# Embedding projection in plain fp32 between the out-projection's outputs, its operands split earlier, norm roots taken on token rows

## The chip, the cores and the metric

The kernel runs on one core of a Trainium2 chip. The metric is the device time of one execution, in microseconds (us). The engines are TensorE (PE; weight loads are listed apart as PEld), VectorE (DVE), ScalarE (ACT), GpSimd (POOL) and SyncE (SP), whose queue issues nearly all DMA transfers in program order.

## The reference

Two layers of a decoder trunk for 1024 prompt tokens and 8 x 4 sample tokens with the same weights, all in float32. Each layer, cut to what matters here:

```python
# layer 0: o = gated linear attention(rms_norm(x)); layer 1: o = dilated window attention
x = x + o @ w_o                                  # out-projection, 1024 x 1024
h = rms_norm(x, g_f)
x = x + (silu(h @ w_gate) * (h @ w_up)) @ w_fo   # SwiGLU, hidden width 22 x 128
h = rms_norm(x, g_e)
x = x + sigmoid(h @ w_eg) * (p[layer] @ w_ep)    # p: 256 numbers per token; w_ep: 256 x 1024
```

## The kernel before

All activations lie transposed: 8 k-tiles of 128 features (partitions) by T = 1056 tokens, so a tile is 128x1056 and a matmul takes one 128x128 weight tile and a third of the tokens, 352 columns. For accuracy each operand of the large products is split into a high and a low part in the format fp32r (`split`: ACT casts the high part, DVE subtracts for the low part), and a product takes three matmuls: high by high, high by low, low by high (`XH,whi`, `XL,whi`, `XH,wlo`). The few plain float32 matmuls (`ones` by `ssq`, transposes) take their operands unsplit.

`block` runs once per layer, in stages:

- The out-projection comes in two halves of four k-tiles each. The first half (`mix_out`, or the end of `mixer` in layer 1) runs while attention still finishes on other engines; its sums with the residual go to DRAM (`Xp`). For the second half the operands O4 to O7 are loaded (`ot`) and split, and the sums come back as `X[m]`. Eight outputs m, in the order 0, 4, 1, 5, 2, 6, 3, 7, take 36 matmuls each. `second` adds an output to X, stores it (`Xr`), squares it into `ssq` and scales it by the norm's weight.
- `gated` computes SwiGLU's hidden tiles by a seven-product scheme after Strassen: a 2x2 split of weights (`seven_weights`) and tokens (`seven_tokens`, after every output m > 3, for the pair k = m - 4 and m). Each of 22 hidden tiles takes 7 products (`al`, `be`, `ga`) of 24 matmuls of 264 columns. Before the first of them stands `norm_done`: the sum over features as a matmul of `ones` by `ssq`, then root and reciprocal on all 128 partitions.
- The down projection takes the hidden tiles back from DRAM (`Gd`, loaded into `gr`) in chunks of 4, 4, 4, 4, 3, 3. In the last chunk X is renormed on the way (`renorm`, `square_sum`).
- The gate stage: `w_eg` by X, eight outputs of 72 matmuls, times the embedding projection `embed(m)`: 18 matmuls from split `p` (pH, pL) and split `w_ep`. Three embeds stand in the last chunk (`EP_AT`), five in the gate stage.

Tiles come from rotating pools, and a scheduler orders the instructions of each engine ahead of time; each engine then runs its own list in order, and semaphores hold an instruction until its operands are there and its buffer is free.

Of the kernel before, what the change touches and what calls it, by code (L numbers as in the profile page):

```python
# [8 lines left out]
F32 = mybir.dt.float32  # L9
# [26 lines left out]
def yoco_step_kernel(  # L36
# [62 lines left out]
    rstd = const.tile([128, T], F32, name="rstd")  # L99

# [21 lines left out]
    Xp = [dr.tile([128, T], F32, name=f"Xp{k}") for k in range(KT)]  # L122
# [21 lines left out]
    def seven_weights(pool, src1, src2):  # L144
# [15 lines left out]
        nc.vector.tensor_tensor(s2, s1, a11, op=ALU.subtract)  # L160
        out[6] = parts(6, s2)
        nc.vector.tensor_tensor(s3, a11, a21, op=ALU.subtract)
        out[7] = parts(7, s3)
        out[5] = parts(5, s1)
        out[4] = parts(4, a22)
        nc.vector.tensor_tensor(s4, a12, s2, op=ALU.subtract)
        out[3] = parts(3, s4)
        return out


    def seven_tokens(x1, x2, tiles, temp):
        a, b = slice(0, HT), slice(HT, T)
        t12, t34 = temp("t12"), temp("t34")
        nc.vector.tensor_tensor(t12[:, a], x1[:, b], x1[:, a], op=ALU.subtract)
        nc.vector.tensor_tensor(t12[:, b], x2[:, b], t12[:, a], op=ALU.subtract)
        bo = tiles("B1")
        split(bo[:, a], bo[:, b], x1[:, a])
        out = {1: (bo[:, a], bo[:, b])}
        nc.vector.tensor_tensor(t34[:, a], x2[:, b], x1[:, b], op=ALU.subtract)
        nc.vector.tensor_tensor(t34[:, b], x2[:, a], t12[:, b], op=ALU.subtract)  # L180
        for x, n1, n2 in ((t12, 5, 6), (x2, 2, 3), (t34, 7, 4)):
            hi, lo = tiles("Bh"), tiles("Bl")
            split(hi, lo, x)
            out[n1], out[n2] = (hi[:, a], lo[:, a]), (hi[:, b], lo[:, b])
        return out
# [354 lines left out]
    def mix_out(half, src, w_o, hl, get, evac, other=None):  # L540
        H_, L_ = hl
        for k in range(4):
            t = get("ot")
            nc.sync.dma_start(t, src[4 * half + k])
# [7 lines left out]
    def gated(i, pool, X7, temp):  # L552

        with ExitStack() as st:
# [9 lines left out]
            for j in range(NH):  # L564
                w = seven_weights(pool, w_fi[i, j], w_fi[i, NH + j])
# [22 lines left out]
    def block(i, sx, src, w_o, gla_scope=None):  # L588
        def first(m, s, ps):
            x = et("xf")  # L590
            nc.sync.dma_start(x, x_t[m])
            nc.vector.tensor_tensor(v3(x), ps, v3(x), op=ALU.add)
            nc.sync.dma_start(Xp[m], x)

        if gla_scope is not None:
            st, et, rest = gla_scope
            mix_out(0, src, w_o, (XH, XL), et, first, (AFTER, rest))
            st.close()
        xp = sx.enter_context(tc.tile_pool(name="xp", bufs=8, side="right"))
        sb, sw = ExitStack(), ExitStack()  # L600
        bg = sb.enter_context(tc.tile_pool(name="bg", bufs=12, side="right"))
        w7 = sw.enter_context(tc.tile_pool(name="w7", bufs=1))
# [4 lines left out]
        def bt(name, dtype=F32):  # L607
            return bg.tile([128, T], dtype, tag="b", name=name)

        X = {}  # L610
        ssq, X7 = bt("ssq"), {}

        def second(m, s, p):
# [4 lines left out]
            if m == 0:  # L618
                nc.scalar.activation(ssq, X[m], AF.Square)
            else:  # L620
                t = bt("sq")
                nc.scalar.activation(t, X[m], AF.Square)
                nc.vector.tensor_tensor(ssq, ssq, t, op=ALU.add)
            nc.scalar.activation(X[m], X[m], AF.Copy, scale=gcol(G_F[i] + m))
            if m > 3:
                k = m - 4
                if k == 3:
                    norm_done(ssq)
                left = [7, 0, 7, 2][k]

                def tile_(name):
                    nonlocal left
                    left -= 1
                    return xtile(name) if left >= 0 else bt(name, F32R)

                X7[k] = seven_tokens(X[k], X[m], tile_, xt if k else bt)

        H_, L_ = ([xtile(f"O{a}{k}") for k in range(4)] for a in "HL")
        for k in range(4):
            t = xtile("ot", F32)  # L640
            nc.sync.dma_start(t, src[4 + k])
            split(H_[k], L_[k], t)
        for m in range(KT):
            X[m] = xt(f"X{m}")
            nc.sync.dma_start(X[m], Xp[m])
        for m in (0, 4, 1, 5, 2, 6, 3, 7):
            for s, p in pieces(wtile(w_o[m][:, 512:], 4), H_, L_, m == 7):
                second(m, s, p)
# [3 lines left out]
        gated(i, w7, [X7[k] for k in range(4)], xt)  # L652
# [8 lines left out]
        X = [xt(f"X{m}") for m in range(KT)]  # L661
        pe = {}

        def embed(m):
            ps = proj(wtile(w_ep[i, m], 2), pH, pL)
            pe[m] = tmp("pe")
            nc.scalar.copy(v3(pe[m]), ps)

        m0 = 0
        for n in FCH:  # L670
            last = m0 + n == NH
            GH, GL = [], []
            for a in range(n):
                t = tmp("gr")
                nc.sync.dma_start(t, Gd[m0 + a])
                GH.append(bt("GH", F32R) if last else xtile("GH"))
                GL.append(bt("GL", F32R) if last else xtile("GL"))
                split(GH[a], GL[a], t)
            if m0 == 0:
                for m in range(KT):  # L680
                    nc.sync.dma_start(X[m], Xr[m])
            if last:
                new_x()
                pH, pL = ([bt(a, F32R) for _ in range(2)] for a in ("pH", "pL"))
                for k in range(2):
                    t = tmp("pt")
                    nc.sync.dma_start(t, p_t[i, k])
                    split(pH[k], pL[k], t)
            for m in range(KT):
# [7 lines left out]
                if last and m in EP_AT:  # L697
                    embed(EP_AT.index(m))
# [4 lines left out]
        for m in range(KT):  # L703
            if m not in pe:
                embed(m)
# [11 lines left out]
        sb.close()  # L717
# [356 lines left out]
    def mixer(mq):  # L1074

        with ExitStack() as st:
# [13 lines left out]
            hp = st.enter_context(tc.tile_pool(name="hp", bufs=1, side="right"))  # L1090
            H_ = [hp.tile([128, T], F32R, name=f"OH{k}") for k in range(4)]
            L_ = [hp.tile([128, T], F32R, name=f"OL{k}") for k in range(4)]
            for k in range(4):
                t = hp.tile([128, T], F32, tag="ot", name="ot", bufs=4)
                nc.sync.dma_start(t, Ad[k])
                split(H_[k], L_[k], t)
            for m in range(KT):
                x = hp.tile([128, T], F32, tag="xf", name="xf", bufs=4)
                nc.sync.dma_start(x, Xd[m])
                for c, ps in mx.proj(wtile(w_ob[m][:, :512], 4), H_, L_):  # L1100
                    s = slice(c * CW, (c + 1) * CW)
                    nc.vector.tensor_tensor(x[:, s], ps, x[:, s], op=ALU.add)
                nc.sync.dma_start(Xp[m], x)


    open_products()
    open_x()
    scope = gla(*load_x())
    sx = ExitStack()
    X, ssq, tp = block(0, sx, Od, w_oa, gla_scope=scope)  # L1110
# [3 lines left out]
    mixer(mq)  # L1114
    mq_stack.close()
    open_products()
    open_x()
    block(1, sx, Ad, w_ob)
    sx.close()
    xh_stack.close()  # L1120
# [116 lines left out]
```

## Time and profile before

| what | value |
|---|---|
| median of 3 runs | 3000.31 us (2995.72 to 3001.23) |
| the profiled execution | 3000.49 us |
| its span | 2998.7 us |
| PE busy | 2902.7 us, 97% |
| DVE busy | 1866.5 us, 62% |
| ACT busy | 1095.9 us, 37% |
| mean DMA rate | 97 GB/s |
| mean granted clock of TensorE | 0.988 |

The span runs from the first to the last instruction; the rest of the time lies around it. PE bounds the kernel as a whole, so what can be saved lies in its instructions and in the places where it waits. The granted clock is a share of 2.4 GHz: 0.50 is 1.2 GHz, the lower of TensorE's two levels.

### The profile page before, as it was taken

Reading aid. Unit: us, or ns where it says so; the run is one execution under the profiler, and the core shown is the slowest. Engines: PE = TensorE matmul, PEld = TensorE weight load, DVE = VectorE, ACT = ScalarE, POOL = GpSimd, SP = SyncE. Lnnn points to the kernel's source line nnn. Section 1 sums busy time; section 2 is a strip of 40 time slices with the busy share of each in tenths; the row PEclk is TensorE's granted clock in tenths of the full one; section 3 lists DMA queues with packets and bytes.
Section 4 is the critical chain, followed back from the end, with each engine's and each line's share of the span. In section 5 each row is a group of like instructions: output and inputs, shape, how many; then the busy total and the mean of one; then the engine's idle time right before and its main releaser. Section 6 shows DMA issues by size and latency. Waiting matters only on the chain.

```text
span 2998.7 us, 47341 instructions
## 1 busy us (share of the span) xinstructions
PE 2902.7 (97%) x19956; PEld 2770.8 (92%) x19956; DVE 1866.5 (62%) x2787; ACT 1095.9 (37%) x1777; POOL 20.3 (1%) x44
## 2 busy tenths in 40 slices
PE   8999998899999999999999999988899999999999
PEld 7889898899999999999988889887799999999999
DVE  6344455866666444557687778773876666545363
ACT  5333343422222221335455555552532222222142
POOL 0000000000000000000000000000000000000000
PEclk9999999999999999999999999999999999999999
DMA  3121245222222532122433141336222222343112
GB/s 128 58 73 50 73 140 208 93 79 86 72 79 82 188 113 64 54 77 90 132 95 107 54 121 43 114 109 236 100 79 79 86 72 79 128 153 104 45 61 77
DMA packets 133989, 291.08 MB, mean 97 GB/s; under 512 B 34160, under 2 KB 58736, under 8 KB 132752
## 3 DMA queue, kind: packets, MB, share of 16 engines
q1 hardware_dynamic: 133040, 287.72, 29.1%
q8 instruction: 157, 2.57, 0.4%
q14 instruction: 56, 0.46, 0.1%
q10 hardware_dynamic: 736, 0.33, 0.0%
HBM read 216.14 MB, written 71.86 MB: 96 GB/s over the span
## 4 chain that ended last, share of the span: by engine, by line
PE 85%; DVE 8%; DMA 3%; ACT 2%; issue 1%; SPq 0%; DVEq 0%; ACTq 0%
PE mm L239 39%; PE be L194 12%; PE ga L194 8%; PE al L194 8%; PE mm L869 6%; PE p_s L916 1%; PE mm L257 1%; PE p_o L984 1%; DVE q L741 1%; DVE hs L749 1%; DVE hs L750 1%; DVE q L751 1%; DVE Bl L134 1%; PE p_u L467 1%; PE p_us L485 1%
## 5 line engine op out<-in xcount | busy, mean ns | idle before, releaser
L133 ACT CAST whi<-raw 128x1024 fp32r<-128x1024 f32 (+3 forms) x260 | 203.9, 784 | 815.2 <-PE mm L239 580.7
L134 DVE TENSOR_TENSOR wlo<-raw,whi 128x1024 fp32r<-128x1024 f32 (+3 forms) x260 | 231.2, 890 | 75.4 <-ACT whi L133 75.2
L239 PE MATMUL mm<-XH,whi 128*128 128x352 f32 x1200 | 271.3, 331 | 0.4 <-ACT q_in L263 0.4
L239 PE MATMUL mm<-XL,whi 128*128 128x352 f32 x1200 | 265.4, 327 | 0.0
L239 PE MATMUL mm<-XH,wlo 128*128 128x352 f32 x1200 | 264.0, 326 | 0.0
L692 DVE TENSOR_TENSOR X<-mm,X 128x1056 f32<-128x1056 f32 (+1 forms) x100 | 121.1, 1212 | 218.4 <-PE mm L239 218.4
L239 PE MATMUL mm<-GH,whi 128*128 128x352 f32 x1038 | 225.3, 326 | 10.7 <-ACT GH L133 10.7
L133 ACT CAST hw<-S 128x512 fp32r<-128x512 f32 x176 | 109.3, 622 | 329.1 <-PE ga L194 181.0
L239 PE MATMUL mm<-GL,whi 128*128 128x352 f32 x1038 | 224.5, 325 | 0.0
L239 PE MATMUL mm<-GH,wlo 128*128 128x352 f32 x1038 | 224.1, 324 | 0.0
L194 PE MATMUL be<-Bh,lw 128*128 128x264 f32 x1056 | 216.2, 286 | 5.9 <-DVE lw L134 5.9
L194 PE MATMUL be<-Bh,hw 128*128 128x264 f32 x1056 | 216.4, 286 | 1.8 <-ACT hw L133 1.7
L194 PE MATMUL be<-Bl,hw 128*128 128x264 f32 x1056 | 216.7, 287 | 0.0
L239 PEld LDWEIGHTS mm<-XH,whi 128*128 128x128 f32 x1200 | 205.3, 189 | 9.1 <-issue 2.5
L239 PEld LDWEIGHTS mm<-XL,whi 128*128 128x128 f32 x1200 | 205.3, 189 | 3.2 <-issue 1.3
L239 PEld LDWEIGHTS mm<-XH,wlo 128*128 128x128 f32 x1200 | 204.1, 189 | 2.2 <-issue 1.6
L869 PE MATMUL mm<-XL,whi 128*128 128x352 f32 x576 | 193.6, 336 | 0.0
L869 PE MATMUL mm<-XH,whi 128*128 128x352 f32 x576 | 193.2, 335 | 0.0
L869 PE MATMUL mm<-XH,wlo 128*128 128x352 f32 x576 | 188.9, 328 | 0.0
L239 PEld LDWEIGHTS mm<-GH,whi 128*128 128x128 f32 x1038 | 177.8, 190 | 11.7 <-ACT GH L133 11.7
L239 PEld LDWEIGHTS mm<-GL,whi 128*128 128x128 f32 x1038 | 177.4, 189 | 0.5 <-DVE GL L134 0.4
L239 PEld LDWEIGHTS mm<-GH,wlo 128*128 128x128 f32 x1038 | 177.1, 189 | 0.0
(340 smaller groups left out, 6212.7 us busy)
## 6 DMA issues: line engine op xcount, KB each, us to landing
raw<-in_w_fi_dram SPq DMA_DIRECT2D x88, 512.0 KB, 3.5
Gd<-g SPq DMA_DIRECT2D x44, 528.0 KB, 2.7
gr<-Gd SPq DMA_DIRECT2D x44, 528.0 KB, 4.7
raw<-in_w_fo_dram SPq DMA_DIRECT2D x64, 256.0 KB, 2.7
raw<-in_w_a_dram SPq DMA_DIRECT2D x24, 512.0 KB, 3.5
raw<-in_w_q_dram SPq DMA_DIRECT2D x24, 512.0 KB, 3.8
kk<-in_ck_dram SPq DMA_DIRECT2D x40, 256.0 KB, 3.2
vv<-in_cv_dram SPq DMA_DIRECT2D x40, 256.0 KB, 3.0
```

The source lines that it names most:

```text
L133: nc.scalar.copy(hi, x)
L134: nc.vector.tensor_tensor(lo, x, hi.bitcast(F32), op=ALU.subtract)
L194: nc.tensor.matmul(ps[:, c, :HC], a[:, k, :], b[:, c * HC:(c + 1) * HC], start=(first and k == 0 and i == 0), stop=(k == len(xs) - 1 and i ...
L239: nc.tensor.matmul(ps[:, c, :CW], a[:, k, :], b[k][:, c * CW:(c + 1) * CW], start=(k == 0 and i == 0), stop=(k == n - 1 and i == 2),)
L257: nc.tensor.matmul(ps, a[:, k, :], b[k][:, s], start=(k == 0 and i == 0), stop=(k == n - 1 and i == 2))
L467: nc.tensor.matmul(p, kr[:, j], vt[:, j], start=True, stop=True)
L485: nc.tensor.matmul(p, kr[q, 8], vm[q], start=True, stop=True, tile_position=(16 * j, 0))
L692: nc.vector.tensor_tensor(like(X[m], s, p), p, like(X[m], s, p), op=ALU.add)
L741: nc.vector.scalar_tensor_tensor(dst[:, :NP].rearrange("p (r u) -> p u r", r=4)[:, u], q[:, :e].rearrange("p (u r) -> p u r", r=4), g, t[: ...
L749: nc.vector.stream_shuffle(t[32:64], dst[:32], [(a + 16) % 32 for a in range(32)])
L750: nc.vector.tensor_tensor(t[:32], t[32:64], tab[32:64], op=ALU.mult)
L869: nc.tensor.matmul(ps, a[:, k, :], b[k][:, s], start=(k == 0 and i == 0), stop=(k == n - 1 and i == 2))
```

## The change

- `embed(m)` takes the raw `w_ep` and the raw `p`, as six plain float32 matmuls of 352 columns, and stands behind the outputs of the out-projection's second half: two behind the first, one behind each of the next six, none behind the last. ACT copies it out, it goes to DRAM (`Pd`) and comes back in the gate stage (`load_pe`). The embeds in the last chunk and the gate stage go.
- The first half's sums stay in SBUF: `first_half` and `mixer` open X's pool themselves; `Xp` goes.
- O4, O5 and O6 are loaded and split at the end of the first half (`out_split`). O7 follows at the second half's beginning.
- `norm_spread` takes the place of `norm_done` ahead of SwiGLU: nine matmuls of `ssq` blocks by one column of ones give the sums with tokens on partitions (128x9, `p_c`); root and reciprocal run on that (`rcol`); nine matmuls of `ones` by diagonal matrices (`dg`) spread them over 128 partitions (`p_r`), and ACT copies them into `rstd`.
- `seven_weights` and `seven_tokens` become generators, so that the first hidden tile's operands are made in pieces: the token sums one output later than before (`later`), the weights around the last output and the norm.
- The first chunk's four G tiles are loaded into X's pool (`GS`) before the SwiGLU weights' pool is released. In the mixer the O tiles are staged in the queries' buffers (tag `q`).

```diff
+    def norm_spread(ssq, dg, n=D):
+        blocks = [(j, min(128, T - 128 * j)) for j in range(9)]
+        p = sm.tile([128, 9], F32, tag="sm", name="p_c")
+        for j, m in blocks:
+            nc.tensor.matmul(p[:m, j:j + 1], ssq[:, 128 * j:128 * j + m], ones[:, :1], start=True, stop=True)
+        for r, c in ((slice(0, 128), slice(0, 8)), (slice(0, 32), slice(8, 9))):
+            nc.scalar.activation(rcol[r, c], p[r, c], AF.Sqrt, scale=1.0 / n, bias=epsb[r])
+            nc.vector.reciprocal(rcol[r, c], rcol[r, c])
+        nc.vector.tensor_tensor(dg[:, :NP].rearrange("p (j n) -> p j n", j=8), ident[:, None, :].to_broadcast([128, 8, 128]),
+                                rcol[:, :8, None].to_broadcast([128, 8, 128]), op=ALU.mult)
+        nc.vector.tensor_tensor(dg[:32, NP:], ident[:32, :32], rcol[:32, 8:9].to_broadcast([32, 32]), op=ALU.mult)
+        for g in range(3):
+            s = slice(512 * g, min(T, 512 * g + 512))
+            q = sm.tile([128, 512], F32, tag="sm", name="p_r")[:, :s.stop - s.start]
+            for j, m in blocks[4 * g:4 * g + 4]:
+                nc.tensor.matmul(q[:, 128 * j - s.start:128 * j - s.start + m], ones[:m], dg[:m, 128 * j:128 * j + m], start=True, stop=True)
+            nc.scalar.copy(rstd[:, s], q)
...
+    def first_half(et, rest):
...
         for m in range(KT):
-            for s, p in pieces(wtile(w_o[m][:, half * 512:half * 512 + 512], 4), H_[:4], L_[:4], half == 1 and m == 7):
-                evac(m, s, p)
-            if other and m == other[0]:
-                other[1]()
+            nc.sync.dma_start(X[m], x_t[m])
+            for s, p in pieces(wtile(w_oa[m][:, :512], 4), H_, L_, False):
+                nc.vector.tensor_tensor(v3(X[m]), p, v3(X[m]), op=ALU.add)
+            if m == AFTER:
+                rest()
+        for k in range(3):
+            out_split(Od[4 + k], H2[k], L2[k], et)
+        return xp, X, H2, L2
...
+        L_ = L_ + [lt("OL7", F32R)]
+        out_split(src, H_[3], L_[3], lt)
+        ps_ = [lt(f"p{k}") for k in range(2)]
+        for k in range(2):
+            nc.sync.dma_start(ps_[k], p_t[i, k])
...
+        def embed(m):
+            raw = raws.tile([128, 1024], F32, tag="raw", name="raw")
+            nc.sync.dma_start(raw[:, :256], w_ep[i, m])
+            ps = mm.tile([128, 3, 512], F32, tag="mm", name="mm")
+            for k in range(2):
+                for c in range(3):
+                    nc.tensor.matmul(ps[:, c, :CW], raw[:, 128 * k:128 * k + 128], ps_[k][:, c * CW:(c + 1) * CW],
+                                     start=(k == 0), stop=(k == 1))
+            t = lt("pe")
+            nc.scalar.copy(v3(t), ps[:, :, :CW])
+            nc.sync.dma_start(Pd[8 * i + m], t)
...
+        for n, m in enumerate((0, 4, 1, 5, 2, 6, 3, 7)):
+            w = wtile(w_o[m][:, 512:], 4)
+            if n == 7:
+                weights = seven_weights(w0, w7, w_fi[i, 0], w_fi[i, NH])
+                next(weights)
+            for s, p in pieces(w, H_, L_, n == 7):
+                second(m, s, p)
+            if later is not None:
+                for _ in tokens(later):
+                    pass
+                later = None
             if m > 3:
...
+                later = m - 4
+            for e in ((0, 1), (2,), (3,), (4,), (5,), (6,), (7,), ())[n]:
+                embed(e)
+        last = tokens(3)
+        next(last)
+        next(last)
+        dg = xt("dg")
+        norm_spread(ssq, dg)
+        next(weights)
+        next(last)
+        next(weights)
...
+        GS = []
+        for a in range(FCH[0]):
+            t = xt("gr")
+            nc.sync.dma_start(t, Gd[a])
+            GS.append(t)
         sw.close()
...
             for k in range(4):
-                t = hp.tile([128, T], F32, tag="ot", name="ot", bufs=4)
-                nc.sync.dma_start(t, Ad[k])
-                split(H_[k], L_[k], t)
+                out_split(Ad[k], H_[k], L_[k], lambda name: mx.pool.tile([128, T], F32, tag="q", name=name, bufs=QB))
```

The order on PE in layer 0's second half. In the kernel before, one output ends and the next begins like this (OH_3720 to OH_3723 are O4 to O7, high parts; each row is three column pieces):

```order
L239 MATMUL mm<-OH_3722,wlo 128x352 x3
L239 MATMUL mm<-OH_3723,whi 128x352 x3
L239 MATMUL mm<-OL_3727,whi 128x352 x3
L239 MATMUL mm<-OH_3723,wlo 128x352 x3
L239 MATMUL mm<-OH_3720,whi 128x352 x3
L239 MATMUL mm<-OL_3724,whi 128x352 x3
```

In the changed kernel the same place reads as follows (OH_3321 to OH_3324 are O4 to O7; p_3752 and p_3753 are the two k-tiles of p):

```order
L271 MATMUL mm<-OL_3327,whi 128x352 x3
L271 MATMUL mm<-OH_3323,wlo 128x352 x3
L271 MATMUL mm<-OH_3324,whi 128x352 x3
L271 MATMUL mm<-OL_3747,whi 128x352 x3
L271 MATMUL mm<-OH_3324,wlo 128x352 x3
L671 MATMUL mm<-p_3752,raw 128x352 x3
L671 MATMUL mm<-p_3753,raw 128x352 x3
L271 MATMUL mm<-OH_3321,whi 128x352 x3
```

An embed of six plain matmuls has moved in between two outputs. The order on DVE at the tail in layer 0, before (X_3758 is the last output's tile, X_3750 its partner, S the sums of weight blocks; L614 is the last output's add, L623 the add to ssq):

```order
L614 TENSOR_TENSOR X_3758<-mm,X_3758 128x352
L174 TENSOR_TENSOR t_4229<-X_3750 128x528
L134 TENSOR_TENSOR B_4233<-X_3750,B_4233 128x528
L623 TENSOR_TENSOR ssq<-ssq,sq 128x1056
L159 TENSOR_TENSOR S_4265<-raw 128x512
L162 TENSOR_TENSOR S_4267<-raw 128x512
L160 TENSOR_TENSOR S_4266<-S_4265,raw 128x512
L134 TENSOR_TENSOR lw<-S_4265,hw 128x512
L134 TENSOR_TENSOR lw<-raw,hw 128x512
L221 RECIPROCAL rstd<-rstd 128x352 x3
L175 TENSOR_TENSOR t_4229<-X_3758,t_4229 128x528
```

And in the changed kernel (X_3312 is the last output's tile, X_3308 its partner):

```order
L678 TENSOR_TENSOR X_3312<-mm,X_3312 128x352
L687 TENSOR_TENSOR ssq<-ssq,sq 128x1056
L163 TENSOR_TENSOR S_4365<-raw 128x512
L244 RECIPROCAL rcol<-rcol 128x8
L244 RECIPROCAL rcol<-rcol 32x1
L164 TENSOR_TENSOR S_4366<-S_4365,raw 128x512
L245 TENSOR_TENSOR dg<-ident,rcol 128x1024
L191 TENSOR_TENSOR t_4321<-X_3312,t_4321 128x528
L247 TENSOR_TENSOR dg<-ident,rcol 32x32
L135 TENSOR_TENSOR lw<-S_4366,hw 128x512
L194 TENSOR_TENSOR t_4322<-X_3312,X_3308 128x528
```

The three wide reciprocals are gone, two narrow ones and the diagonals stand in their place, and the first token sums (L190) have moved ahead of the last add. The order on SP at the mixer's end, before (Ad holds the attention's outputs):

```order
L228 DMA raw<-in_w_ob_dram 128x512
L1095 DMA ot<-Ad_140 128x1056
L1095 DMA ot<-Ad_141 128x1056
L1095 DMA ot<-Ad_142 128x1056
L1095 DMA ot<-Ad_143 128x1056
L1099 DMA xf<-Xd_86 128x1056
L909 DMA scr<-stA 128x8x2
```

And in the changed kernel (Xd holds the residual, stX and scr belong to the sample tokens' attention):

```order
L575 DMA ot<-Ad_149 128x1056
L1165 DMA X_19031<-Xd_87 128x1056
L1165 DMA X_19032<-Xd_88 128x1056
L1165 DMA X_19033<-Xd_89 128x1056
L260 DMA raw<-in_w_ob_dram 128x512
L1165 DMA X_19034<-Xd_90 128x1056
L575 DMA ot<-Ad_150 128x1056
L977 DMA scr<-stA 128x8x2
L1165 DMA X_19035<-Xd_91 128x1056
L1165 DMA X_19036<-Xd_92 128x1056
L993 DMA stX<-scr 128x2x8
L575 DMA ot<-Ad_151 128x1056
```

The four loads, which stood together, are now spread among the loads of X.

## Rows read from the trace of the kernel before

**Rows 1.** The page's first part: busy time, share of the span, instructions.

```profile
PE 2902.7 (97%) x19956; PEld 2770.8 (92%) x19956; DVE 1866.5 (62%) x2787; ACT 1095.9 (37%) x1777; POOL 20.3 (1%) x44
```

**Rows 2.** What PE waited for, whole span: total us, times, longest.

```profile
PE mm L239 <- ACT OH L133: 12.5, 1, 12.5
PE mm L239 <- ACT GH L133: 10.7, 4, 4.9
PE mm L239 <- ACT whi L133: 8.9, 1, 8.9
...
PE be L194 <- DVE lw L134: 5.9, 1, 5.9
PE mm L239 <- DVE wlo L134: 4.7, 3, 2.9
PE al L194 <- DVE Bl L134: 3.5, 1, 3.5
...
PE mm L239 <- DVE X L614: 2.7, 3, 1.2
PE p_n L219 <- DVE ssq L623: 2.7, 2, 2.2
PE mm L869 <- DVE OL L134: 2.6, 1, 2.6
...
PE al L194 <- DVE B L134: 2.1, 1, 2.1
...
PE ga L194 <- ACT hw L133: 1.7, 1, 1.7
...
PE mm L257 <- DVE X L614: 1.5, 1, 1.5
```

**Rows 3.** Windows, PE: us, busy us (instructions), granted clock, DMA share, GB/s; nine stretches.

```profile
484.10:489.15 5.05, 5.05 (x17) 0.50 0.26 97
516.46:519.87 3.41, 3.41 (x13) 0.50 0.50 154
...
2617.99:2622.49 4.50, 4.50 (x15) 0.50 0.98 306
sum 45.21, PE 40.23; mean PE 4.47
```

**Rows 4.** Windows: PE, PEld, DVE, ACT, POOL busy us (instructions), clock, DMA share, GB/s.

```profile
484.10:538.90 54.80, 50.66 (x288) 50.11 (x289) 38.39 (x45) 28.95 (x33) 0.00 (x0) 0.92 0.35 122
538.90:558.00 19.10, 9.86 (x59) 7.63 (x57) 19.10 (x21) 10.72 (x15) 0.00 (x0) 0.90 0.15 57
1285.00:1386.00 101.00, 101.00 (x631) 101.00 (x630) 52.14 (x49) 36.49 (x39) 0.00 (x0) 1.00 0.26 90
600.00:700.00 100.00, 100.00 (x822) 100.00 (x821) 67.19 (x93) 27.09 (x38) 0.00 (x0) 1.00 0.24 81
```

**Rows 5.** Timeline of PE: start us, length us, line, operation, count.

```profile
444.36 1.34 PE L510 MATMUL p_n<-os,ones 128*128 128x352 f32 x4
445.28 0.92 PE L239 MATMUL mm<-XH,whi 128*128 128x352 f32 x3
446.03 0.65 PE L239 MATMUL mm<-XL,whi 128*128 128x352 f32 x3
```

**Rows 6.** Timeline of DVE at the tail of layer 0.

```profile
548.89 6.77 DVE L221 RECIPROCAL rstd<-rstd 128x352 f32<-128x352 f32 x3
```

**Rows 7.** Groups by line, last chunk, DVE: count, busy us, mean ns, idle before.

```profile
L692 DVE TENSOR_TENSOR X<-mm,X 128x1056 f32<-128x1056 f32 x14 | 17.6, 1256 | 22.1 <-PE mm L239 22.1
L137 DVE SCALAR_TENSOR_TENSOR XL<-X,gt,XH 128x1056 fp32r<-128x1056 f32 x7 | 9.2, 1319 | 5.5 <-ACT XH L136 5.5
L213 DVE TENSOR_TENSOR ssq<-ssq,sq 128x1056 f32<-128x1056 f32 x7 | 8.8, 1254 | 1.2 <-ACT sq L212 1.2
L134 DVE TENSOR_TENSOR wlo<-raw,whi 128x384 fp32r<-128x384 f32 x13 | 7.1, 550 | 0.1
```

**Rows 8.** The page's DMA issues: count, KB each, us from issue to landing.

```profile
gr<-Gd SPq DMA_DIRECT2D x44, 528.0 KB, 4.7
```

More of the change, by code (lines that the diff above doesn't have):

```diff
@@ L99, in yoco_step_kernel @@
     rstd = const.tile([128, T], F32, name="rstd")
+    rcol = const.tile([128, 16], F32, name="rcol")
     def gcol(i):
@@ L148, in seven_weights @@
         a11, a12, a21, a22 = r1[:, :512], r1[:, 512:], r2[:, :512], r2[:, 512:]
+        hi, lo = (wp.tile([128, 8, 128], F32R, tag=t, name=t) for t in ("whi", "wlo"))
+        split(*(t[:].rearrange("p k m -> p (k m)") for t in (hi, lo)), r1)
+        out[1], out[2] = (hi[:, :4], lo[:, :4]), (hi[:, 4:], lo[:, 4:])
+        yield
+        pool = get()
         s1, s2, s3, s4 = (pool.tile([128, 512], F32, tag=f"S{n}", name=f"S{n}") for n in range(1, 5))
@@ L586, in gated, with block, lt, w7 @@
                 nc.sync.dma_start(Gd[j], g)
[L588 to L602, printed above, removed]
+    def block(i, xp, X, H_, L_, src, w_o, pick):
+        sw = ExitStack()
+        lstack = ExitStack()
+        lp = lstack.enter_context(tc.tile_pool(name="lt", bufs=6))
+        def lt(name, dtype=F32):
+            return lp.tile([128, T], dtype, tag="t", name=name)
         def xt(name):
             return xp.tile([128, T], F32, tag="X", name=name)
[L607 to L611, printed above, removed]
+        pw = []
+        def w7():
+            if not pw:
+                lstack.close()
+                pw.append(sw.enter_context(tc.tile_pool(name="w7", bufs=1)))
+            return pw[0]
+        L_ = L_ + [lt("OL7", F32R)]
[3 more added lines that the diff above has]
+            nc.sync.dma_start(ps_[k], p_t[i, k])
+        ssq = lt("ssq")
+        X7 = [{} for _ in range(4)]
+        def embed(m):
[9 more added lines that the diff above has]
+            nc.sync.dma_start(Pd[8 * i + m], t)
         def second(m, s, p):
@@ L624, in second, with tokens @@
             nc.scalar.activation(X[m], X[m], AF.Copy, scale=gcol(G_F[i] + m))
-            if m > 3:
[L626 to L648, printed above, removed]
+        def tokens(k):
+            return seven_tokens(X7[k], X[k], X[k + 4], lambda name: pick(k, name), xt if k else lt)
+        w0 = {}
+        later = None
[8 more added lines that the diff above has]
+                for _ in tokens(later):
+                    pass
+                later = None
+            if m > 3:
+                later = m - 4
[9 more added lines that the diff above has]
+        next(weights)
         mma_stack.close()
         mmb_stack.close()
-        gated(i, w7, [X7[k] for k in range(4)], xt)
+        gated(i, w0, w7(), X7, xt)
+        GS = []
[3 more added lines that the diff above has]
+            GS.append(t)
         sw.close()
@@ L659, in tmp, with load_pe @@
             return tp.tile([128, T], F32, tag=tag, name=name, bufs=bufs)
-        X = [xt(f"X{m}") for m in range(KT)]
         pe = {}
-        def embed(m):
-            ps = proj(wtile(w_ep[i, m], 2), pH, pL)
+        def load_pe(m):
             pe[m] = tmp("pe")
-            nc.scalar.copy(v3(pe[m]), ps)
+            nc.sync.dma_start(pe[m], Pd[8 * i + m])
         m0 = 0
@@ L673, in block @@
             for a in range(n):
[L674 to L677, printed above, removed]
+                if m0:
+                    t = tmp("gr")
+                    nc.sync.dma_start(t, Gd[m0 + a])
+                else:
+                    t = GS[a]
+                GH.append(pick("last" if last else "chunk", "GH"))
+                GL.append(pick("last" if last else "chunk", "GL"))
                 split(GH[a], GL[a], t)
             if m0 == 0:
+                X = [xt(f"X{m}") for m in range(KT)]
                 for m in range(KT):
@@ L682, in block @@
             if last:
[L683 to L688, printed above, removed]
+                XH[:] = [pick("XH", f"XH{k}") for k in range(KT)]
+                XL[:] = [pick("XL", f"XL{k}") for k in range(KT)]
             for m in range(KT):
@@ L1113, in yoco_step_kernel, with in_op, in_bg2, pick1 @@
     close_products()
-    mixer(mq)
+    xp, op, X = mixer(mq)
+    bg2 = sx.enter_context(tc.tile_pool(name="bg2", bufs=20, side="right"))
+    def in_op(name):
+        return op.tile([128, T], F32R, tag="o", name=name)
+    def in_bg2(name, dtype=F32R):
+        return bg2.tile([128, T], dtype, tag="b", name=name)
+    H_, L_ = [in_bg2(f"OH{k}") for k in range(4, 8)], [in_bg2(f"OL{k}") for k in range(4, 7)]
+    for k in range(3):
+        out_split(Ad[4 + k], H_[k], L_[k], lambda name: in_bg2(name, F32))
     mq_stack.close()
     open_products()
-    open_x()
-    block(1, sx, Ad, w_ob)
+    n2 = [1]
+    def pick1(what, name):
+        if what in (0, "XH"):
+            return in_op(name)
+        if what == 1 and n2[0]:
+            n2[0] -= 1
+            return in_op(name)
+        return in_bg2(name)
+    block(1, xp, X, H_, L_, Ad[7], w_ob, pick1)
     sx.close()
-    xh_stack.close()
     close_products()
```

107 lines of the change are left out of this document (63 added, 44 removed).

## The prediction, made blind

> **What bounds the kernel now.** I read the share of each engine first: TensorE (PE) is busy for 2902.7 of 2998.7 us, DVE for 62% [rows 1]. So the time is PE's instructions plus what PE waits, and only two things can shorten it: fewer or cheaper matmuls, or shorter waits. Next I took the view of what PE waits for [rows 2]. Its largest waits stand at four places, each of which occurs once per block; the lines say which:
> - the start of the out-projection's second half, where O4 to O7 are loaded and split: 12.5 (OH) and 8.9 (whi, late behind those loads in SP's queue), 21.4 us;
> - inside the second half, where an output waits for DVE: 4.7 + 2.7 + 1.5 = 8.9;
> - the tail between out-projection and SwiGLU, where the last output is squared, the norm root taken and the first seven-product operands split: 5.9 + 3.5 + 2.7 + 2.1 + 1.7 + 1.7 = 17.6 (of the two alike for hw, one stands in the rows);
> - the first chunk of the down projection, where G comes back from DRAM (GH): 10.7.
>
> That is 58.6 us. A wait also costs afterwards. I asked for the granted clock of the stretches behind them: nine show 0.50, which is 1.2 in place of 2.4 GHz, and PE works 40.2 us in them [rows 3]. At 0.50 it started 17 matmuls in 5.05 us, 0.297 each; at 1.00 it started 631 in 101.0, 0.160 each [rows 3, 4]. So 46% of working time at 0.50 is lost: 18.5 us. The nine lie two at the second half's start (9.6 us of PE's work), two inside it (6.8), three at the tail (15.5) and two at the chunk's start (8.3), so the loss is 4.4, 3.1, 7.1 and 3.8. The four places together hold 58.6 + 18.5 = 77.1 us.
>
> **The change, part by part.**
>
> *Embedding, plain fp32.* Before, an output takes 18 matmuls of 352 columns (two k-tiles, three products, three column pieces), at the 0.160 above: sixteen outputs, 288 matmuls, 46.1 us. After, 96 plain ones. Their price stands in the trace: four records of the plain ones matmul (L510) and three split ones take 446.03 - 444.36 = 1.67 us, so 1.67 - 3 x 0.160 = 1.19 for four, 0.297 a record; a plain matmul leaves two records, 0.594 us [rows 5]. 96 x 0.594 = 57.0, so **+10.9 us**. The Trainium skill, "FP8 and Floating Point Precision", section "TensorE Precision Notes", counts four passes for true FP32, which at 0.160 a pass would be 61.4 us and the sum 4.4 higher; the rows show a little less than four, and I keep them. ACT's and DVE's splits of p and w_ep go; they lay under PE's work, and I count them at nothing.
>
> *Operands split in the first half; X kept in SBUF.* The loads and splits of O4 to O6 now come under the first half's matmuls, and Xp's stores and reloads leave SP's queue. What is left is O7, needed only by an output's last quarter. In block 1 the loads of O4 to O7 must follow the stores of Ad, and should end some us before PE gets there. I take the whole start, **-(21.4 + 4.4) = -25.8**. Bounds: all of it, or half, if O7 and its split are late.
>
> *Embeds between outputs.* An output of 36 matmuls takes 36 x 0.160 = 5.8 us of PE; with one embed, 5.8 + 6 x 0.594 = 9.4. In the second half DVE was busy 38.4 of 54.8 us and ACT 29.0 [rows 4]. After, the same DVE work and eight copies more on ACT lie under 8 x 9.4 = 75 us. The waits inside come from DVE being late by 1 to 3 us when an odd output's seven-token sums stand ahead of the next add; the embed behind each output gives 3.6 us. I take **-(8.9 + 3.1) = -12.0**, and keep as the other end that half stays.
>
> *The tail.* Three reciprocals of 352 columns, 6.77 us on DVE [rows 6], become two on 8 and 1 columns. The rest of DVE's 19.1 us there [rows 4], when it was never idle, shrinks also because 75 us rather than 55 have passed. By the order shown above, with t = 0 at the end of the last output: PE does product 1, 24 matmuls of 264 columns at 100/822 = 0.122 [rows 4], until 2.9. p_c needs ssq: a third of X's add (0.4), its Square (as X's add, 1.26), the ssq add 1.25 [rows 7] and hand-overs, about 3.6; wait 0.7. p_c's nine matmuls have no row; between nothing and nine plain ones of 352 columns (5.3) I take them by columns as 9 x 0.594 x 128/352 = 1.9, and p_r's nine likewise. So p_c ends near 5.6. Then the second product needs S2's cast, on ACT behind two roots, a cast and X's scaling, by the widths 0.6 + 0.6 + 1.2 + 0.6 us: 8.5, wait 2.9. Afterwards the pieces arrive about as PE wants them. So 3.6 us of waits stay per block, with 2.0 of clock behind them (4.4 us at 0.50): **-(17.6 + 7.1) + 2 x 5.6 = -13.5**. PE's own norm work grows from 3 x 0.594 = 1.8 to 3.9 us a block, **+4.2**. Bounds: nothing gained here, and 11.2 more.
>
> *First chunk.* Four G tiles are loaded into xp's buffers before the pool of SwiGLU weights is released, so the 4.7 us of gr<-Gd [rows 8] lie under the last products, except for the last tile's. I leave 0.5 a block: **-(10.7 + 3.8) + 1.0 = -13.5**.
>
> *Where embeds stood.* In the last chunk (three k-tiles) an output takes PE 27 x 0.160 = 4.32 us and DVE 1.256 + 1.319 + 1.254 + 0.550 = 4.38 [rows 7]. Three embeds gave DVE slack there. Now nothing does: between 0 and 3 us a block, I take 1, **+2.0**. In the gate stage PE had no waits and loses only the embeds' matmuls.
>
> *The mixer's end.* O0 to O3 of block 1 are staged in the queries' four buffers, of which three are in use, so three loads wait for queries and stand on SP behind loads of X (order above). Today PE waits 2.6 there for OL [rows 2]. A load is 3 to 5 us, and a second and third in turn could cost 8 to 10; if queries come free early, nothing. I take **+3.0**.
>
> **Sum.** 10.9 - 25.8 - 12.0 - 13.5 + 4.2 - 13.5 + 2.0 + 3.0 = -44.7. The profiled execution took 3000.5 us (span 2998.7, 1.8 around it), 0.2 above the median of the runs, so the two need no correction: **2955.8 us**. What measurement can tell from no change here is about 0.2%, 6 us.
>
> **Rivals.**
> 1. *Hand-overs in the second half.* ACT and DVE pass tiles to and fro in each odd output, and PE may find its buffer unread. For it: before, waits of this kind added to 8.9 us and two of the nine stretches at 0.50 follow them [rows 2]. Against it: 3.6 us more cover per output. With 1.3 us of wait and one more stretch of 3.41 us at 0.50 (1.57 lost) [rows 3] at each of the eight odd outputs it adds 8 x 2.9 = 23: 2979. The Trainium skill, "TensorE: Matmul & The Clock Gate", section "A second HAM failure mode: psum-queue depth-cycling", says that brief idling between groups of matmuls, repeated, keeps the clock falling and rising though no single pause is long. By that rule the clock's part of this rival, 8 x 1.57 = 12.6 us, would come even from pauses shorter than 1.3; whether the trace agrees in this pattern no row shows, since the outputs stood back to back.
> 2. *Slower: weights late behind Pd's stores.* A store of Pd waits in SP's queue for ACT's copy, and the weight loads behind it can't be issued. Were each of 14 outputs to wait 2.9 us (the longest wlo wait, as in the 4.7 of [rows 2]) with 1.57 of clock, 63 us come back: 3019. It decides from 3.2 us per output. Against it: the order has each weight load about two outputs ahead, 18 us, and such a load lands in some 3.
> 3. *The waits only move.* Tail and chunk start stay as they were, because DVE is the bound there for other reasons: both terms of 13.5 are taken back, 2955.8 + 27 = 2982.8.
> 4. *Everything hidden.* The tail's 11.2, the chunk's 1, the mixer's 3 and the last chunk's 2 don't occur, 17 us: 2939.
> 5. *No change to speak of.* Rival 1 at twice its price, 46 us: about 3000.
>
> **How the numbers follow.** Chances: the forecast, with a range of its own of 2944 to 2968 (the tail and mixer at either end), 0.58; rival 1 0.16; rival 2 0.05; rival 3 0.07; rival 4 0.10; rival 5 0.04. The predicted time is the forecast's. Leaving out rivals 2 and 5 and the edges of 1 and 4, the range is 2935 to 2984. Faster by over 0.2%: all but rivals 2 and 5, 0.91; within: rival 5, 0.04; slower: 0.05.
>
> **What would show it.** In the profile after: PE's waits for OH and whi at the second half's start under 2 us; the second half lasting about 75 us with a clock of 1.00; the embeds' records 0.297 us apart; a tail with one wait of about 3 us ahead of the second product, no 6.77 us of reciprocals; no wait for GH of 4.9. I am wrong if the second half shows a wait at each output (rivals 1, 2), if the waits at Ad's reload or at the mixer's end exceed 10 us, or if plain matmuls with a new weight tile for every three cost more than 0.594.

## The result, and the profile after

The changed kernel takes 2963.97 us, median of 4 runs (2961.08 to 2967.59), against 3000.35 for the kernel before (4 runs): a ratio of 0.9882 with a 95% interval of 0.9865 to 0.9900, or 36 us less. The forecast was 2955.8, with a range of 2935 to 2984. The profiled execution was the slowest of the four; its span is 2965.8 us, 32.9 below that of before.

The page's first part, as in [rows 1]:

```profile
PE 2909.5 (98%) x19920; PEld 2762.0 (93%) x19920; DVE 1845.1 (62%) x2769; ACT 1085.1 (37%) x1761; POOL 19.9 (1%) x44
```

PE's busy time grew by 7 us while the span fell by 33: what went is waiting. What PE still waits for, over the whole span (the view of [rows 2]: total us, times, longest):

```profile
PE be L207 <- ACT hw L134: 5.2, 2, 2.6
PE p_os L1127 <- DMA vv<-in_cv_dram: 5.1, 5, 1.8
PE mm L271 <- DVE wlo L135: 4.7, 2, 2.3
PE p_ss L1083 <- DMA kk<-in_ck_dram: 4.4, 6, 0.9
PE p_t L1041 <- DVE pA L1038: 3.3, 3, 1.4
...
PE mm L937 <- DVE OL L135: 3.0, 2, 2.6
PE p_c L241 <- DVE ssq L687: 1.5, 2, 0.8
```

The waits of L239 for OH, GH and whi, together 32.1 us in [rows 2], are no longer there. New is a wait for wlo, twice 2.3 us. It isn't that of the second half, as its place will show. The second half runs from 475.58 to 550.83 in layer 0 and to 2143.8 in layer 1. Windows of both halves' PE work, then of two stretches at the lower clock (columns as in [rows 4]):

```profile
475.58:550.83 75.25, 75.13 (x386) 64.50 (x386) 43.67 (x49) 39.54 (x43) 0.00 (x0) 1.00 0.43 157
...
2066.00:2143.80 77.80, 77.80 (x403) 67.38 (x403) 44.48 (x51) 39.83 (x43) 0.00 (x0) 1.00 0.43 154
558.12:564.95 6.83, 4.85 (x22) 4.61 (x22) 6.31 (x12) 4.69 (x7) 0.00 (x0) 0.50 0.01 2
1274.92:1278.33 3.41, 3.41 (x9) 2.42 (x8) 2.04 (x2) 0.87 (x2) 0.00 (x0) 0.50 0.76 219
```

In the first two PE is busy throughout at a clock of 1.00, where [rows 4] had 0.92 and 50.7 busy of 54.8 us. The embeds themselves, in PE's timeline:

```profile
481.39 7.26 PE L671 MATMUL mm<-p,raw 128*128 128x352 f32 x24
488.56 0.75 PE L271 MATMUL mm<-OH,whi 128*128 128x352 f32 x3
```

Two embeds are 24 records in 488.56 - 481.39 = 7.17 us, 0.299 a record and 3.59 us an embed; the forecast had 0.297 and 3.56. At the tail, PE waits 0.8 us for ssq and 2.6 us for the cast hw (the high part of S):

```profile
555.42 2.10 PE L241 MATMUL p_c<-ones,ssq 128*128 128x1 f32 x18 [0.76 <-DVE ssq L687]
560.10 0.59 PE L207 MATMUL be<-Bh,hw 128*128 128x264 f32 x1 [2.58 <-ACT hw L134]
560.49 3.62 PE L252 MATMUL p_r<-dg,ones 128*128 128x128 f32 x16
```

Both waits were forecast, as 0.7 and 2.9, and p_c's matmuls take 2.10 us where 1.9 was estimated. ACT's timeline shows the last link, which is the one that I had forecast: from p_c's end at 557.55 on it does two roots, a cast and X's scaling without a pause, and only then the cast of S, whose first half ends near 560.05.

```profile
557.55 0.40 ACT L243 ACTIVATE rcol<-p_c,epsb 128x8 f32<-128x8 f32 x2 [3.48 <-PE p_c L241]
557.86 0.60 ACT L134 CAST hw<-raw 128x512 fp32r<-128x512 f32 x1
558.37 1.17 ACT L688 ACTIVATE X<-X,gt 128x1056 f32<-128x1056 f32 x1
559.45 1.12 ACT L134 CAST hw<-S 128x512 fp32r<-128x512 f32 x2
```

DVE's timeline at the same place shows what I had not seen, why this chain could not begin earlier:

```profile
554.11 1.26 DVE L687 TENSOR_TENSOR ssq<-ssq,sq 128x1056 f32<-128x1056 f32 x1 [1.15 <-ACT sq L686]
557.55 0.69 DVE L163 TENSOR_TENSOR S<-raw 128x512 f32<-128x512 f32 x1 [2.19 <-PE p_c L241]
...
558.31 0.67 DVE L164 TENSOR_TENSOR S<-S,raw 128x512 f32<-128x512 f32 x1
```

The first weight sum S waited until p_c was done, though its operands come from DRAM and have nothing to do with the norm. The third place is the gate stage's start. PE first, then DVE:

```profile
1270.81 0.65 PE L271 MATMUL mm<-XL,whi 128*128 128x352 f32 x3
1273.81 0.75 PE L271 MATMUL mm<-XH,wlo 128*128 128x352 f32 x3 [2.35 <-DVE wlo L135]
```

```profile
1267.28 0.53 DVE L764 TENSOR_TENSOR X<-mm,X 128x352 f32<-128x352 f32 x1
...
1269.51 0.95 DVE L764 TENSOR_TENSOR X<-mm,X 128x352 f32<-128x352 f32 x2
...
1271.54 1.08 DVE L138 SCALAR_TENSOR_TENSOR XL<-X,gt,XH 128x352 fp32r<-128x352 f32 x2
1272.53 1.22 DVE L135 TENSOR_TENSOR wlo<-raw,whi 128x1024 fp32r<-128x1024 f32 x1
```

DVE works without a pause up to 1272.53 and only then comes to the low part of the first gate weights; PE waits 2.35 us for it and then runs 3.41 us at 0.50. Neither the load nor ACT is late here: the high part that wlo needs was cast by 1265.93.

```profile
1264.88 1.05 ACT L134 CAST whi<-raw 128x1024 fp32r<-128x1024 f32 x1 [0.43 <-PE mm L271]
```

The same happens in layer 1.

### The profile page after: what moved, and what is told of

It reads as the page before. It is cut to its first block, busy times and chain, and to the rows that moved or that the text cites. A ratio compares the mean times of both kernels' runs of the same rounds, so it can differ in the third digit from the quotient of the medians.

```text
span 2965.8 us, 47230 instructions
## 1 busy us (share of the span) xinstructions
PE 2909.5 (98%) x19920; PEld 2762.0 (93%) x19920; DVE 1845.1 (62%) x2769; ACT 1085.1 (37%) x1761; POOL 19.9 (1%) x44
## 4 chain that ended last, share of the span: by engine, by line
PE 88%; DVE 6%; DMA 3%; ACT 2%; issue 1%; SPq 0%; DVEq 0%; ACTq 0%
PE mm L271 38%; PE be L207 13%; PE ga L207 9%; PE al L207 8%; PE mm L937 6%; PE mm L671 2%; PE p_s L984 1%; PE p_o L1052 1%; PE mm L289 1%; DMA vv<-in_cv_dram 1%; DMA kk<-in_ck_dram 1%; DVE hs L817 1%; DVE q L809 1%; PE p_s L973 1%; DVE q L819 1%
## 5 line engine op out<-in xcount | busy, mean ns | idle before, releaser
L134 ACT CAST whi<-raw 128x1024 fp32r<-128x1024 f32 (+2 forms) x244 | 197.6, 810 | 789.3 <-PE mm L271 578.5
L135 DVE TENSOR_TENSOR wlo<-raw,whi 128x1024 fp32r<-128x1024 f32 (+2 forms) x244 | 224.6, 921 | 80.0 <-ACT whi L134 79.9
L271 PE MATMUL mm<-XH,wlo 128*128 128x352 f32 x1104 | 245.3, 328 | 4.7 <-DVE wlo L135 4.7
L271 PE MATMUL mm<-XH,whi 128*128 128x352 f32 x1104 | 249.3, 331 | 0.2 <-ACT q_in L295 0.2
L271 PE MATMUL mm<-XL,whi 128*128 128x352 f32 x1104 | 247.3, 328 | 0.2 <-DVE XL L138 0.2
L271 PEld LDWEIGHTS mm<-XH,wlo 128*128 128x128 f32 x1104 | 189.0, 190 | 8.0 <-DVE wlo L135 5.3
L271 PEld LDWEIGHTS mm<-XH,whi 128*128 128x128 f32 x1104 | 188.6, 189 | 8.2 <-issue 3.1
L271 PEld LDWEIGHTS mm<-XL,whi 128*128 128x128 f32 x1104 | 190.2, 189 | 4.1 <-issue 1.3
L937 PE MATMUL mm<-XL,whi 128*128 128x352 f32 x576 | 193.7, 336 | 0.0
L937 PE MATMUL mm<-XH,whi 128*128 128x352 f32 x576 | 193.7, 336 | 0.0
L937 PE MATMUL mm<-XH,wlo 128*128 128x352 f32 x576 | 189.3, 329 | 0.0
```

The lines of the kernel that those rows point to most:

```text
L134: nc.scalar.copy(hi, x)
L135: nc.vector.tensor_tensor(lo, x, hi.bitcast(F32), op=ALU.subtract)
L271: nc.tensor.matmul(ps[:, c, :CW], a[:, k, :], b[k][:, c * CW:(c + 1) * CW], start=(k == 0 and i == 0), stop=(k == n - 1 and i == 2),)
L937: nc.tensor.matmul(ps, a[:, k, :], b[k][:, s], start=(k == 0 and i == 0), stop=(k == n - 1 and i == 2))
```

## The experiments

Each runs beside the kernel before on the same chip, so I compare ratios to it; 0.001 is 3.0 us. The changed kernel has 0.9880 to 0.9882. A difference between two of the ratios is uncertain by some 6 to 8 us.

| kernel | median us | ratio to before, 95% interval |
|---|---|---|
| the changed kernel, again | 2964.55 | 0.9880 (0.9863 to 0.9896) |
| all embeds back, plain | 2979.91 | 0.9931 (0.9913 to 0.9948) |
| all embeds back, split | 2960.70 | 0.9870 (0.9850 to 0.9890) |
| one embed back | 2954.41 | 0.9847 (0.9832 to 0.9861) |
| late splits | 2965.50 | 0.9882 (0.9865 to 0.9900) |
| X's trip | 2978.04 | 0.9924 (0.9910 to 0.9937) |
| X's trip and late splits | 2990.86 | 0.9969 (0.9960 to 0.9978) |
| old norm | 2980.49 | 0.9931 (0.9911 to 0.9950) |
| late G | 2981.51 | 0.9937 (0.9918 to 0.9956) |
| ssq apart | 2958.81 | 0.9860 (0.9847 to 0.9874) |
| one embed back, ssq apart | 2948.92 | 0.9827 (0.9812 to 0.9841) |

**Both kernels, profiled again.** No edit.

> The changed kernel as it is, profiled a second time. Between the mixer's first scores and its first O matmul its engines run the same instructions in the same order as the kernel before, yet its first profile shows 471.2 us there against 463.5. If that is variation of the cache loads and small transfers from one execution to the next, this profile gives anything from 463 to 471 and the waits for kk, vv and pA change; if it is a lasting effect of the change, it gives 471 again. The time stays within 2961 to 2968 in either case.

> The kernel before, profiled a second time, for the same question: if the mixer's length varies from execution to execution, it may come out anywhere from 463 to 471; if the changed kernel lengthens it for good, this one shows 463 to 464 again.

The mixer's length, from the first p_s to the first OH matmul, came out as 469.2 us for the changed kernel (471.2 the first time) and 466.9 for the one before (463.5). The changed kernel's first profile, for the two ends of that stretch:

```profile
1514.75 0.82 PE L973 MATMUL p_s<-KA,q 128*128 128x128 f32 x4
```

```profile
1985.99 0.58 PE L937 MATMUL mm<-OH,whi 128*128 128x352 f32 x2 [0.99 <-ACT OH L134]
```

In twelve profiles of the changed kernel and its variants it lies between 464.7 and 473.0. These twelve have the same instructions in the same order there (the kernel before differs from them in SP's last loads, of O and X), so such a stretch scatters by some 8 us. The waits for kk, vv and pA (cached keys and values, and scaled scores) make up a good part of it: 6.0 to 11.4 us in the twelve. Of the two of before one length lies within the scatter and one just below it, and their waits, 4.1 and 5.4 us, are below those of all twelve. That speaks for a small lasting loss, some 3 us, but two profiles don't show it.

**Where the embeds stand.** All of them back, as plain fp32, p loaded again for them:

```diff
-            for e in ((0, 1), (2,), (3,), (4,), (5,), (6,), (7,), ())[n]:
-                embed(e)
...
+                if last and m in {3: 0, 5: 1, 6: 2}:
+                    embed({3: 0, 5: 1, 6: 2}[m], tmp)
...
-            load_pe(m)
+            if m not in pe:
+                embed(m, tmp)
...
```

> All embeds go back to the last chunk (three) and the gate stage (five), still as plain fp32; the rest of the change stays. If the place between the outputs matters as cover for DVE, the second half has waits again, about the 12.0 us over both blocks of the kernel before, the tail grows by some 6, and the gate stage's 7.8 go: about 2974. If the early splits alone took the second half's waits away, nothing comes back and only the 7.8 go: about 2956.

It takes 2979.9 us, 15 more, near what cover for DVE gives. What PE waits for in layer 0's second half and tail:

```profile
PE al L207 <- DVE B L135: 2.7, 1, 2.7
PE be L207 <- ACT hw L134: 2.6, 1, 2.6
PE mm L271 <- DVE wlo L135: 2.3, 1, 2.3
...
PE mm L271 <- DVE X L682: 0.8, 1, 0.8
```

X and wlo inside the second half and B at the tail are the waits of [rows 2] again, though the operands were split early; none of them is in the changed kernel (its waits for hw, 2.6 us, are there in both). At the gate stage's start the 2.35 us are gone.

The same with the embeds as they had been, split in fp32r:

```diff
-            ps = mm.tile([128, 3, 512], F32, tag="mm", name="mm")
-            for k in range(2):
-                for c in range(3):
-                    nc.tensor.matmul(ps[:, c, :CW], raw[:, 128 * k:128 * k + 128], ps_[k][:, c * CW:(c + 1) * CW],
-                                     start=(k == 0), stop=(k == 1))
...
+            ps = proj(wtile(w_ep[i, m], 2), pH, pL)
...
```

> The embeds as they were before the change (split in fp32r, 18 matmuls, in the last chunk and the gate stage), with the rest of the change. PE does 10.9 us less than with plain embeds at the same places, whatever those give; with waits back in the second half and the tail (+18) and the gate stage's 7.8 gone it is about 2963, no slower than the changed kernel. If the plain form's price were not on the path, it would equal the kernel with plain embeds at the old places.

2960.7 us, and a ratio of 0.9870: not distinguishable from the changed kernel. Against plain embeds at the same places it is 0.0061 less, 18 us, where 10.9 was expected; the two intervals leave some 10 to 26. PE's busy time is 2911.1 us in the one profile and 2900.5 in the other, 10.6 apart. So plain fp32 costs PE what it should, and the place between the outputs earns about as much as that form and the gate stage's new wait cost. The move of the embeds, as it was made, brought nothing on balance.

One embed back, behind the last chunk's sixth output:

```diff
-            for e in ((0, 1), (2,), (3,), (4,), (5,), (6,), (7,), ())[n]:
+            for e in ((1,), (2,), (3,), (4,), (5,), (6,), (7,), ())[n]:
...
+                if last and m in {5: 0}:
+                    embed({5: 0}[m], tmp)
...
```

> One embed of eight (number 0) goes from the second half back to the last chunk, behind its sixth output, still as plain fp32; p is loaded again for it. If the gate stage's wait for wlo (2.35 us a block, and 3.41 us at a clock of 0.50 behind it) comes from DVE having no slack in the last chunk, 3.6 us of PE work there take it away: 2 x 3.9 = 7.8 us less, about 2956. If it comes from the load of w_eg or from ACT, the wait stays and the time is about 2964. If the second embed behind the first output was cover for the operands of the outputs after it, a new wait of 1 to 3 us a block shows in the second half.

2954.4 us, 10 less, and the window around the gate stage's start is full at a clock of 1.00:

```profile
1255.00:1300.00 45.00, 45.00 (x265) 43.09 (x265) 34.97 (x32) 23.35 (x26) 0.00 (x0) 1.00 0.36 116
```

The wait and the stretch at 0.50 behind it are gone in both layers. With the load and ACT's cast done 6.6 us before DVE's turn, it was DVE's lack of slack. One embed is cover enough behind the second half's first output too: the stretch to the tail shows no wait over 0.31 us.

**The second half's start.** O4 to O7 split late:

```diff
-        for k in range(3):
-            out_split(Od[4 + k], H2[k], L2[k], et)
...
-        out_split(src, H_[3], L_[3], lt)
+        for k in range(4):
+            out_split(src[4 + k], H_[k], L_[k], lt)
...
```

> O4 to O7 are all loaded and split at the beginning of the second half, into buffers of their own; X stays in SBUF, the rest of the change stays. If the early load and split are what took the second half's start away, most of the 25.8 us come back: 2980 to 2990. If it was SP's queue, freed of Xp's stores and reloads, the time stays within 5 us of 2964.

2965.5 us: no change. SP's timeline says why (start, length, line, transfer, count):

```profile
460.14 1.95 SPq L575 DMA_DIRECT2D ot<-Od  x4
```

The loads are issued at 460 to 462 even so, 14 us before they are needed; no store or reload of X stands ahead of them. Next, X goes through DRAM again, with early splits:

```diff
+            nc.sync.dma_start(Xp[m], X[m])
             if m == AFTER:
...
+        for m in range(KT):
+            nc.sync.dma_start(X[m], Xp[m])
...
```

> X makes its way through DRAM again (each of the first half's sums is stored and loaded back), O4 to O6 are split early as in the changed kernel. With late splits alone having cost nothing, my theory is now that the trip of X, which holds up the weight loads behind it in SP's queue, made the wait at the second half's start: then some 8 to 12 us a block come back with their clock, 2980 to 2990. If either of the two parts suffices to take the wait away, this stays within 5 us of 2964.

2978.0 us, 13 more. In layer 0 PE waits 9.0 us for whi, as it did in [rows 2]. SP's timeline, then DVE's, then PE's:

```profile
475.79 0.32 SPq L661 DMA_DIRECT2D X<-Xp  x1
478.55 0.32 SPq L590 DMA_DIRECT2D Xp<-X  x1
478.91 0.43 SPq L664 DMA_DIRECT2D p<-in_p_t_dram  x1
479.39 0.77 SPq L261 DMA_DIRECT2D raw<-in_w_oa_dram  x1
```

```profile
477.27 1.26 DVE L589 TENSOR_TENSOR X<-mm,X 128x1056 f32<-128x1056 f32 x1 [0.97 <-PE mm L272]
```

```profile
486.23 1.25 PE L272 MATMUL mm<-OH,whi 128*128 128x352 f32 x3 [9.00 <-ACT whi L135]
```

The first weight load of the second half goes out at 479.39, behind the store of X's last sum at 478.55, which waits for DVE's add to end at 478.53; PE had been done since 477.23. In layer 1 only 2.1 us of wait come back. And both undone:

> Both undone: X through DRAM and O4 to O7 split late. If the trip alone is the cause, it equals the kernel with X's trip and early splits within 4 us. If the two parts each cover for the other, only this one shows the 25.8 us, about 2990.

2990.9 us, 26 more, against the forecast's 25.8 for the whole term. The waits at the second half's start are 11.7 us in layer 0, where PE turns to an embed first, and 7.8 us in layer 1:

```profile
PE mm L674 <- DMA raw<-in_w_ep_dram: 11.7, 1, 11.7
...
PE mm L272 <- ACT whi L135: 7.8, 1, 7.8
```

So X's trip is the part that costs: with it the early splits are worth 13 us, without it nothing.

**The tail and the first chunk.** The norm ahead of SwiGLU as before:

```diff
-        dg = xt("dg")
-        norm_spread(ssq, dg)
+        norm_done(ssq)
```

> The norm ahead of SwiGLU as before the change (three matmuls, roots and reciprocals on 352 columns of 128 partitions), the rest of the change stays. If the reciprocals' 6.8 us on DVE set the tail, it grows by some 4 to 6 us a block with the clock behind it, less 2.1 of PE's work: 2968 to 2974. If the reciprocals were hidden under the products that follow, only PE's 4.2 us go: 2960.

2980.5 us, 15 more, above what was expected. The waits of layer 0's tail:

```profile
PE al L207 <- ACT u L616: 4.7, 1, 4.7
PE be L207 <- ACT hw L134: 4.0, 1, 4.0
```

They are 9.7 us in all in place of 3.8, and in layer 1 9.9 in place of 4.2: 11.6, less PE's 4.2, gives 7.4 for the two tails. The clock adds nothing to that: the stretches at 0.50 are longer, 10.24 in place of 6.83 us each, but PE works about as much in the two together (10.3 against 11.0 us). The rest isn't the norm's by anything that the profile shows: 3.9 us more lie between the mixer's first OH matmul and the end of layer 1's second half, where PE waits longer for kk and once 1.5 us for whi. The two ratios leave 7 to 23 us for the difference, so 7.4 alone is just possible. And the first chunk's G loaded late:

```diff
-        GS = []
-        for a in range(FCH[0]):
-            t = xt("gr")
-            nc.sync.dma_start(t, Gd[a])
-            GS.append(t)
...
```

> The first chunk's four G tiles are loaded after the SwiGLU weights' pool is released, as before the change. The wait of 4.9 us a block for GH and its clock come back if the early buffers took it away: +13.5, about 2977. If the wait had another cause, such as the order of SP's queue, the time stays near 2964.

2981.5 us, 17 more; the wait for GH is back in the size of [rows 2]:

```profile
PE mm L271 <- ACT GH L134: 10.8, 4, 5.1
```

**The wait that stays at the tail.** The sum of squares in rstd's own tile, the last square in one of X's:

```diff
-        ssq = lt("ssq")
+        ssq = rstd
...
-                t = lt("sq")
+                t = xt("sq") if m == 7 else lt("sq")
```

> The sum of squares lies in rstd's own tile and the last square in one of X's buffers, so that the SwiGLU weights' pool, which reuses the memory of the pool that held ssq, need not wait for p_c. In the changed kernel's profile DVE's first sum S waited 2.2 us for p_c. If that reuse is what keeps 2.6 us of wait ahead of the second product, S and its cast come earlier, the wait goes below 1 us and the clock does not fall: 4 to 11 us less, 2953 to 2960. If ACT's queue (roots, cast, scaling), as I predicted, sets the wait, it stays at 2.6 and the time at 2964.

2958.8 us, 6 less. S now runs ahead of the add to ssq, in time in which DVE had been idle:

```profile
552.54 0.68 DVE L163 TENSOR_TENSOR S<-raw 128x512 f32<-128x512 f32 x1
...
553.78 1.26 DVE L687 TENSOR_TENSOR rstd<-rstd,sq 128x1056 f32<-128x1056 f32 x1
554.96 0.69 DVE L164 TENSOR_TENSOR S<-S,raw 128x512 f32<-128x512 f32 x1
```

On ACT the cast of the first S now stands ahead of the roots, and behind them PE waits for one cast alone:

```profile
553.66 0.60 ACT L134 CAST hw<-S 128x512 fp32r<-128x512 f32 x1
557.24 0.40 ACT L243 ACTIVATE rcol<-p_c,epsb 128x8 f32<-128x8 f32 x2 [2.98 <-PE p_c L241]
557.54 0.60 ACT L134 CAST hw<-S 128x512 fp32r<-128x512 f32 x1
```

PE's wait for hw falls from 2.58 to 1.00 us in layer 0, with 3.41 us at 0.50 in place of 6.83; in layer 1 it is all but gone (0.16), and its stretch at 0.50 with it. So both had a part: ACT's queue behind the roots is what PE waited for, and the memory's reuse is what kept the weights' sums and casts from going ahead of the roots. The gain of 6 us by itself is no larger than the ratios' uncertainty; it is the rows that carry the reading.

**Both improvements together** (one embed back, ssq apart; no other edit).

> One embed back in the last chunk and the sum of squares apart, together. If the two gains are of different places and add up: 2954 less 4 to 11, 2943 to 2950, faster than both kernels. If the tail's wait stays, 2954.

2948.9 us, a ratio of 0.9827: 52 us below the kernel before and 16 below the changed one. The single gains, 10 and 6, add up, as far as intervals of that width can say: neither the wait for wlo at the gate stage's start nor a wait over 1.0 us for hw is left.

## Why the prediction was right, point by point

The forecast missed by 8 us of 45, in a range that held the time. By its own terms, with the profile's numbers:

| term | forecast | measured | from |
|---|---|---|---|
| embeds, plain | +10.9 | +11.3 | 16 x 3.59 less 46.1 |
| second half's start | -25.8 | -25.8 | no wait there; undone, +26 |
| inside the second half | -12.0 | -12.0 | no wait, clock 1.00 |
| tail's waits | -13.5 | about -12 | 8.0 us of waits stay and, at 46% lost, 5.1 for 11.0 us of PE work at 0.50 |
| norm's own matmuls | +4.2 | +4.6 | p_c 2.10 us; p_r 3.26 and 0.44 us at 0.50, about 2.0 at full clock; less 1.8 |
| first chunk | -13.5 | -14.5 | no wait; undone, +17 |
| last chunk, gate stage | +2.0 | +7.8 | 2 x (2.35 + 1.57) |
| mixer's end | +3.0 | 0 | OL 2.6 us as before |
| mixer | 0 | +7.7 | 471.2 against 463.5; scatter, perhaps some 3 of it lasting |

The measured terms add to about -33, the span's difference is -32.9. The sum leaves little over, but a wait that is gone counts there with the size that it had before.

*Mis-sized: "between 0 and 3 us a block, I take 1".* I had weighed DVE's 4.38 us against PE's 4.32 in the last chunk [rows 7] and looked for the loss there. It appears one stage later: PE goes on, DVE arrives late at the gate stage's first weights, and the clock adds 1.57 to the 2.35. With the embed back it is gone, so cause and size are shown. Taking cover away from an engine that is just in balance is paid where the next new operand has to come from it.

*Right in size, wrong in its reason: the second half's start.* I gave it to the early splits and the freed queue together. The runs separate them: early splits alone are worth nothing, X's trip alone costs 13 us, both together 26.

*Right in size and in the last link: the tail's 2.9 us.* I derived them from ACT's queue, and they were 2.6, at the end of just that chain. What I took as given was that the chain must stand behind p_c: DVE's row at 557.55 and the run with ssq apart show that S and its casts waited for the memory in which ssq lay.

*Rivals.* Rivals 1 and 5 (hand-overs) and rival 2 (weights behind Pd's stores) did not occur: no wait between outputs in either layer. Nor did rival 3: the chunk start's waits went, and of the tail's 17.6 us 8.0 stayed. For the rule on brief idling in the Trainium skill ("TensorE: Matmul & The Clock Gate", section "A second HAM failure mode: psum-queue depth-cycling") this is no test, since PE did not idle: the clock is 1.00 over both stretches. The four passes that the Trainium skill counts ("FP8 and Floating Point Precision", section "TensorE Precision Notes") give, as an estimate at 0.160 a pass, 3.84 us an embed; the trace has 3.59, and the measurement decides. Rival 4 was half right: first chunk and mixer's end cost nothing, the tail and the last chunk did. One sign of being wrong was set too sharply: a plain matmul with new weights for every three takes 0.597 us, 0.003 over the 0.594 named, which is 0.3 us in the whole kernel.

*What stays open.* The mixer's scatter hides whether it has become some 3 us longer. About half of the old norm's 15 us stands at places that have nothing to do with the norm, and one profile can't say whether it would come again.

## What to carry to other kernels

When work is moved to give one engine cover, look at what it covered where it stood: here the embeds held DVE's slack in the last chunk, and putting one of eight back gained 10 us. A store that waits for a late result holds up the loads behind it in the same queue, here the second half's first weights; with that trip gone, splitting the operands early was worth nothing. Reused memory is a dependence like any other: an engine's idle time in front of an instruction whose operands are ready is its sign. A forecast that names the right last link can still take as given what put the chain there.

## What the runs showed of the hardware

A plain float32 matmul of 352 columns leaves two records and takes 0.597 us, 3.7 times the 0.160 of an fp32r one, also when new weights come with every third matmul. The same instructions in the same order took from 464.7 to 473.0 us over the mixer's stretch in twelve profiles of the changed kernel and its variants; the waits that differ most between the first profiles of before and after are those for kk, vv and pA (over the whole span 12.8 us after and 4.9 before).
